# Each 128-row matmul with w_o as two 64-row matmuls side by side in the array

## The chip, the cores and the metric

The kernel runs on one core of a Trainium2 chip. The metric is the device time of one execution in microseconds, the median of several runs. Two kernels that differ by more than about 0.2% can be told apart.

## What is computed

The program is two layers of an encoder trunk over 640 tokens (512 of a new stream, 128 of eight running ones), model width 1024, in fp32. In each layer a half-step feed-forward block is followed by a mixer and a second feed-forward block. What matters here is the end of the mixer and what comes before and after it:

```python
m = g_conv * (y_conv @ w_conv_out) + g_attn * (y_attn @ w_attn_out)
x = x + m @ w_o                                  # the products of this change
x = x + 0.5 * swiglu(rmsnorm(x, norm_ffn2), w_ffn2_gu, w_ffn2_down)
```

## The kernel before

**Numbers.** Activations lie transposed: eight tiles `x[0..7]` of 128 channels x 640 tokens. To keep fp32 precision at the speed of the fp32r type, every operand is split into a rounded part and a remainder (`hi`, `lo`), and each product is three matmuls: hi x hi, lo x hi, hi x lo. The remainder of a weight block is made on VectorE (`wlo`, line 269) from a ScalarE cast (`whi`, line 264), two blocks ahead of its use. `flush()` issues the pending `wlo` subtractions.

**A product.** `steps` (line 327) takes one 128 x 128 weight tile per contraction step; `product` (line 341) runs all of them. With w_o there are 8 contraction steps, 3 terms and 2 token halves of 320 columns: 48 matmuls of 128 rows x 128 columns on 320 tokens (line 337). They accumulate in one PSUM tile `po` of two banks, a bank for each half. The eight output blocks m = 0..7 of a layer are eight such products, 384 matmuls a layer, 768 in all.

**PSUM.** From the gates of the mixer on (`layout(f"g{l}", 1)`, line 954) the eight banks are divided in two pools: `acc` with two buffers of two banks each, and `att` with four buffers of one bank. Each pool hands out its buffers in turn, and the first matmul into a buffer waits until the last reader of its previous content is done.

- The products with w_conv_out and w_attn_out (`out`, line 1071) take `acc` buffers in turn, as `py`; line 1081 reads them on VectorE.
- The products with w_o (lines 962 to 966) took `acc` buffers in turn as well, as `po`; line 966 adds a finished one to `x[m]` on VectorE.
- The three sums of the next block's first `gate_up` (line 709: `pa`, `pb`, `pc`) take `att` buffers.

**Order.** In these stages TensorE, VectorE and ScalarE each run their instructions in the order of the program. The last w_attn_out product is issued with its VectorE work in this order: the remainders of three operands for w_o (`give`, line 182, `m_3lo` to `m_5lo`), then line 1081, an add to `mm`, and the last two remainders `m_6lo`, `m_7lo`. Then follow, for each m, the product, `ex.weights(m)` (which prepares weights of the next block at m = 5 and 7), the add to `x[m]`, the `wlo` of a block two ahead, and `ex.final(m)`: the operands of the next block, made from `x[m]`: about two VectorE steps for an even m, five for an odd one (lines 481 to 514), their squares on ScalarE (line 533), and a running sum of squares (line 208). After m = 7 comes `gate_up`, whose first matmuls read operands of the even blocks, then of the odd ones; a little later the sum of squares is reduced on TensorE (line 427, `npsb`).

Elsewhere the kernel already has matmuls with 64 contraction rows: the attention scores (line 1207), where two heads lie in partitions 0 to 63 and 64 to 127, and each head has a PSUM bank of its own. They are plain fp32.

Of the kernel before, what the change touches and what calls it, by code (L numbers as in the profile page):

```python
# [13 lines left out]
ALU = mybir.AluOpType  # L14
# [9 lines left out]
HT = T // 2  # L24
PAST = 256
H = 8
HD = 64
# [106 lines left out]
def two(ps):  # L134
    return ps[:, :, :HT]


def halves(t):
    return t.rearrange("p (a b) -> p a b", a=2)
# [3 lines left out]
def trunk(ctx: ExitStack, tc: tile.TileContext, xin, wst, small, pbias, samplebias, kcache, vcache,  # L143
          yout, ko, vo, co):
    nc = tc.nc
    PE, DVE, ACT, POOL, SP = nc.tensor, nc.vector, nc.scalar, nc.gpsimd, nc.sync
# [8 lines left out]
    ps = ExitStack()  # L155
# [12 lines left out]
    def acc(name):  # L168
        return banks["acc"].tile([P, 2, 512], F32, tag="acc", name=name)

    def att(name):
        return banks["att"].tile([P, 512], F32, tag="att", name=name)
# [14 lines left out]
    slabs, n = [], 0  # L187
# [19 lines left out]
    def add(out, a, b):  # L207
        DVE.tensor_tensor(out=out, in0=a, in1=b, op=ALU.add)  # L208
# [58 lines left out]
    def flush():  # L267
        for lo, src, hi in pending:
            DVE.tensor_tensor(out=lo, in0=src, in1=hi.bitcast(F32), op=ALU.subtract)  # L269
        pending.clear()  # L270
# [50 lines left out]
    tiles = Tiles()  # L321
# [5 lines left out]
    def steps(ps, ops, at=()):  # L327


        n = len(ops)  # L330
        for k, (xh, xl) in enumerate(ops):
            if k in at:
                at[k]()
            wh, wl = tiles.take()
            for j, (w, x) in enumerate(((wh, xh), (wh, xl), (wl, xh))):
                for a in range(2):
                    PE.matmul(ps[:, a, :HT], w, x[:, a * HT : (a + 1) * HT],  # L337
                              start=k == 0 and j == 0, stop=k == n - 1 and j == 2)
            yield

    def product(ps, ops, at=()):
        for _ in steps(ps, ops, at):
            pass

    def block(ps, s, half, ops, ks, start, stop):

        for kp in ks:
            w = [z[:, (half * NP + kp) * P : (half * NP + kp + 1) * P] for z in s]
            xh, xl = ops(kp)
            for j, (a, b) in enumerate(((w[0], xh), (w[0], xl), (w[1], xh))):  # L350
                PE.matmul(ps, a, b, start=start and kp == 0 and j == 0,  # L351
                          stop=stop and kp == NP - 1 and j == 2, skip_group_check=True)
# [15 lines left out]
    x = [xp.tile([P, T], F32, name=f"x{k}") for k in range(KT)]  # L368
    for k in range(KT):
# [4 lines left out]
        if k % 2 == 0:  # L374
            c = slice(k * P, (k + 2) * P)
# [192 lines left out]
    def opening(fp, name, goff, n, put, tails):  # L568
# [52 lines left out]
        for i in range(2 * n):  # L621
            ps.append(acc(f"po{name}_{i}"))
            product(ps[i], h, at.get(i, {}))
            if i > 1:
                out(i - 1)
            if i == 0:
                for k in range(KT):
                    ex.square(k)
                    ex.add()
                    if k == 1:  # L630
                        out(0)
                    if k == 4:
                        flush()
            if i == 1:
                continue
            if i == 3:
                g, u = gs[0], us[0]
                DVE.tensor_tensor(out=g, in0=g, in1=ex.rho, op=ALU.mult)
                ACT.activation(g, g, AF.Silu)
                DVE.tensor_tensor(out=u, in0=u, in1=ex.rho, op=ALU.mult)  # L640
            flush()
            for m in made.get(i, ()):
                ex.final(m, False)
            if i == 3:
                DVE.tensor_tensor(out=u, in0=u, in1=g, op=ALU.mult)
            if i == max(made):
                ex.rest()
# [176 lines left out]
    def ffn(name, fp, ex, goff, after, end=False):  # L824
# [9 lines left out]
        for what, a in ffn_order(name):  # L834
            if what in ("std", "cut"):
                continue
            if what == "gu":
                turned = after is not None and not end
                gate_up(fp, f"{name}_{a}", ex, a == plain, turned, tails, act.__setitem__, a)
                continue  # L840
            js = a[0][1]
            if js[0] == last or len(a) * len(js) >= KT:
                for t in tails:
                    t()
                tails.clear()
            if after is not None and js[0] == last:
                nxt = nxt or after()
            if end and js[0] == last:
                nxt.all([act[j] for j in js])
                break  # L850
            for m, js in a:
                pd = acc(f"pd{name}_{js[0]}_{m}")
                product(pd, [act[j] for j in js])
                done = nxt and m == KT - 1
                if nxt:
                    nxt.weights(m)
                DVE.scalar_tensor_tensor(out=halves(x[m]), in0=two(pd), scalar=0.5,  # L857
                                         in1=halves(x[m]), op0=ALU.mult, op1=ALU.add)
                if not done:
                    flush()  # L860
                if nxt:
                    nxt.final(m)
# [5 lines left out]
    def mixer(l, after):  # L868
        with tc.tile_pool(name=f"yp{l}", bufs=1, reuse_waits="tile") as yp, \
# [8 lines left out]
            ops = Operands(l, op, h, ycs, [yas[:, c, :] for c in range(1, CT)])  # L878
# [76 lines left out]
            with tc.tile_pool(name=f"gp{l}", bufs=1, reuse_waits="tile") as gp, \  # L955
                 tc.manual_schedule(engines=ORDERED):
                hold[0] = True
                mo = outputs(l, gp, ops.X, st, cs, ycs, yas, sigmoid, gates)
        ex = after(st)
        with tc.manual_schedule(engines=ORDERED):  # L960
            hold[0] = True
            for m in range(KT):
                po = acc(f"po{l}_{m}")
                product(po, mo)
                ex.weights(m)
                DVE.tensor_tensor(out=halves(x[m]), in0=two(po), in1=halves(x[m]), op=ALU.add)
                if m < KT - 1:
                    flush()
                ex.final(m)
# [532 lines left out]
    for l in range(L):  # L1502
        if l == 0:
            open_pool("fp")
            ex = None
        with tc.manual_schedule(engines=ORDERED):
            ffn(f"a{l}", pool[0], ex, O_G1, None)
        fp.close()

        def after(st):  # L1510
            open_pool(f"fp{l}")
            return Expand(pool[0], f"b{l}", O_G2 + l * KT, st)

        ex = mixer(l, after)
        with tc.manual_schedule(engines=ORDERED):
            if l < L - 1:
                ex = ffn(f"b{l}", pool[0], ex, 0,
                         lambda: Expand(pool[0], f"a{l + 1}", O_G1 + (l + 1) * KT, ex))
            else:
                ffn(f"b{l}", pool[0], ex, 0, Final, True)  # L1520
# [128 lines left out]
```

## Time and profile before

| | us |
|---|---|
| median of 3 runs | 2574.79 (2574.21 to 2574.84) |
| the profiled execution | 2574.47 |
| its span, first to last instruction | 2572.7 |
| TensorE busy | 2553.6, 17576 matmuls |
| VectorE busy | 1934.1 |
| ScalarE busy | 1144.7 |
| matmuls with w_o on the chain that ended last | 4.0% of the span |

In rows of the time line the first number is the start in us from the beginning of the span and the second the length in us; then come the engine (PE is TensorE, PEld its weight loads, DVE VectorE, ACT ScalarE), line, operation, output and inputs, shape and count. A bracket gives the idle time of the engine before the row and what ended it. Rows of groups give the busy time of the group in us and the mean length in ns of one. A matmul's length includes its way through the array, so the next one starts well before it ends; the time that a stream of matmuls costs is read from start to start.

### The profile page before, as it was taken

How to read it: one execution, taken by the hardware profiler on the slowest of the kernel's cores; microseconds unless marked ns; L12 is line 12 of the kernel's file. 1: busy time of each engine (PE TensorE's matmuls, PEld its weight loads, DVE VectorE, ACT ScalarE, POOL GpSimd, SP SyncE). 2: the span in 40 equal slices, each digit the busy share in tenths (PEclk: the TensorE clock that was granted, in tenths of full speed). 3: DMA queues.
4: the chain of work that ended last, by engine and by line, in shares of the span. 5: the costliest groups of instructions: out<-in, count | busy, mean ns of one | idle time of the engine just before them, and what ended most of it. 6: DMA issues, size and time to landing. Idle time of an engine off the chain costs nothing.

```text
span 2572.7 us, 42534 instructions
## 1 busy us (share of the span) xinstructions
PE 2553.6 (99%) x17576; PEld 2497.1 (97%) x17576; DVE 1934.1 (75%) x2973; ACT 1144.7 (44%) x1802; POOL 60.5 (2%) x153
## 2 busy tenths in 40 slices
PE   8999999999999999999999999999999999999998
PEld 8999999888999999999999999998889999999998
DVE  7786767778777987677787767787786778777676
ACT  5343335575444543334444333356644445433333
POOL 0000000111000000000000000001110000000000
PEclk9999999999999999999999999999999999999999
DMA  3222223235222232222222222233442222222222
GB/s 133 66 100 91 81 75 108 99 116 168 75 83 88 74 102 74 81 89 78 83 82 99 74 90 83 74 101 113 134 136 83 74 91 81 92 83 74 91 91 74
DMA packets 74066, 237.05 MB, mean 92 GB/s; under 512 B 8241, under 2 KB 19121, under 8 KB 73873
## 3 DMA queue, kind: packets, MB, share of 16 engines
q1 hardware_dynamic: 70272, 223.90, 26.0%
q0 software_dynamic: 2880, 9.79, 1.1%
q8 instruction: 138, 2.26, 0.4%
q10 hardware_dynamic: 720, 0.65, 0.1%
q14 instruction: 56, 0.45, 0.1%
HBM read 225.85 MB, written 7.94 MB: 91 GB/s over the span
## 4 chain that ended last, share of the span: by engine, by line
PE 92%; DVE 4%; ACT 3%; issue 1%; DMA 0%; ACTq 0%; DVEq 0%
PE pab L351 12%; PE pda L337 12%; PE pdb L337 11%; PE paa L351 11%; PE pcb L351 6%; PE pca L351 5%; PE py L337 4%; PE po L337 4%; PE qa L351 4%; PE pbb L351 3%; PE pba L351 3%; PE pv L1160 2%; PE ma_cv L351 2%; PE ma_qk L351 2%; PE qc L351 2%; PE ma_b L351 1%
## 5 line engine op out<-in xcount | busy, mean ns | idle before, releaser
L269 DVE TENSOR_TENSOR wlo<-raw,whi 128x1024 fp32r<-128x1024 f32 (+2 forms) x540 | 562.5, 1047 | 189.5 <-ACT whi L264 187.3
L264 ACT CAST whi<-raw 128x1024 fp32r<-128x1024 f32 (+2 forms) x540 | 489.9, 912 | 253.7 <-PE pca L351 79.4
L351 PE MATMUL pab<-xhib,whi 128*128 128x320 f32 x704 | 218.4, 310 | 0.4 <-ACT u_b L791 0.4
L351 PE MATMUL pab<-xlob,whi 128*128 128x320 f32 x704 | 217.5, 309 | 0.0
L351 PE MATMUL pab<-xhib,wlo 128*128 128x320 f32 x704 | 217.5, 309 | 0.0
L351 PE MATMUL paa<-xhia,whi 128*128 128x320 f32 x640 | 198.2, 310 | 0.7 <-ACT c_a L727 0.5
L351 PE MATMUL paa<-xloa,whi 128*128 128x320 f32 x640 | 197.7, 309 | 0.0
L351 PE MATMUL paa<-xhia,wlo 128*128 128x320 f32 x640 | 197.7, 309 | 0.0
L337 PE MATMUL pda<-ahia,whi 128*128 128x320 f32 x704 | 160.3, 309 | 0.6 <-DVE x L857 0.6
L337 PE MATMUL pda<-ahia,wlo 128*128 128x320 f32 x704 | 160.4, 309 | 0.0
L337 PE MATMUL pda<-aloa,whi 128*128 128x320 f32 x704 | 160.4, 309 | 0.0
L264 ACT CAST whi<-s 128x1024 fp32r<-128x1024 f32 (+1 forms) x120 | 109.5, 912 | 111.8 <-DVE s L208 85.4
L337 PE MATMUL pdb<-ahib,wlo 128*128 128x320 f32 x656 | 149.5, 309 | 0.0
L337 PE MATMUL pdb<-alob,whi 128*128 128x320 f32 x656 | 149.4, 309 | 0.0
L337 PE MATMUL pdb<-ahib,whi 128*128 128x320 f32 x656 | 149.3, 309 | 0.0
L269 DVE TENSOR_TENSOR wlo<-s,whi 128x1024 fp32r<-128x1024 f32 (+1 forms) x120 | 127.2, 1060 | 13.1 <-ACT whi L264 13.1
L351 PEld LDWEIGHTS pab<-xhib,whi 128*128 128x128 f32 x704 | 132.2, 188 | 1.2 <-ACT u_b L791 0.9
L351 PEld LDWEIGHTS pab<-xlob,whi 128*128 128x128 f32 x704 | 132.2, 188 | 0.2
L351 PEld LDWEIGHTS pab<-xhib,wlo 128*128 128x128 f32 x704 | 132.1, 188 | 0.0
L351 PEld LDWEIGHTS paa<-xhia,whi 128*128 128x128 f32 x640 | 120.1, 188 | 1.3 <-ACT c_a L727 0.8
L351 PEld LDWEIGHTS paa<-xloa,whi 128*128 128x128 f32 x640 | 120.1, 188 | 0.1
L351 PEld LDWEIGHTS paa<-xhia,wlo 128*128 128x128 f32 x640 | 120.1, 188 | 0.0
(582 smaller groups left out, 6952.7 us busy)
## 6 DMA issues: line engine op xcount, KB each, us to landing
raw<-in_wst SPq DMA_DIRECT2D x384, 512.0 KB, 3.5
kc<-in_kcache SPq DMA_DIRECT2D x32, 256.0 KB, 4.0
vc<-in_vcache SPq DMA_DIRECT2D x16, 512.0 KB, 4.5
bias<-in_pbias POOLq DMA_DIRECT2D x16, 256.0 KB, 3.2
x<-in_xin SPq DMA_DIRECT2D x8, 320.0 KB, 5.1
out_vo<-v POOLq DMA_DIRECT2D x10, 256.0 KB, 2.5
out_ko<-k POOLq DMA_DIRECT2D x8, 320.0 KB, 2.5
out_yout<-x SPq DMA_DIRECT2D x8, 192.0 KB, 1.9
```

What stands on the lines that cost most here:

```text
L264: ACT.copy(hi[:, d], src[:, c])
L269: DVE.tensor_tensor(out=lo, in0=src, in1=hi.bitcast(F32), op=ALU.subtract)
L337: PE.matmul(ps[:, a, :HT], w, x[:, a * HT : (a + 1) * HT], start=k == 0 and j == 0, stop=k == n - 1 and j == 2)
L351: PE.matmul(ps, a, b, start=start and kp == 0 and j == 0, stop=stop and kp == NP - 1 and j == 2, skip_group_check=True)
L1160: PE.matmul(pv[t], xx[:, t * P : (t + 1) * P], w[:, kk * AW : (kk + 1) * AW], start=c == 0 and kk == 0 and j == 0, stop=c == KT // 2 - 1 a ...
```

## The change

Each matmul of a w_o product becomes two. The first uses weight rows 0 to 63 and the token operand's partitions 0 to 63, the second rows 64 to 127 of both. They lie beside each other in the array, and each has a sum of its own: four PSUM banks for an output block (two row halves x two token halves) in place of two. Even blocks take both `acc` buffers, odd blocks all four `att` buffers. Both sums are added to `x[m]`: two adds of 640 columns for an even block, four of 320 for an odd one, in place of one of 640.

```diff
+    def beside(ps, ops):
+        n = len(ops)
+        for k, (xh, xl) in enumerate(ops):
+            wh, wl = tiles.take()
+            for j, (w, x) in enumerate(((wh, xh), (wh, xl), (wl, xh))):
+                for a in range(2):
+                    for r in range(2):
+                        c = slice(r * HD, (r + 1) * HD)
+                        PE.matmul(ps[r][a], w[c], x[c, a * HT : (a + 1) * HT],
+                                  start=k == 0 and j == 0, stop=k == n - 1 and j == 2)
...
             for m in range(KT):
-                po = acc(f"po{l}_{m}")
-                product(po, mo)
+                if m % 2:
+                    po = [[att(f"po{l}_{m}_{r}{a}")[:, :HT] for a in range(2)] for r in range(2)]
+                else:
+                    pair = [acc(f"po{l}_{m}_{r}") for r in range(2)]
+                    po = [[z[:, a, :HT] for a in range(2)] for z in pair]
+                beside(po, mo)
                 ex.weights(m)
-                DVE.tensor_tensor(out=halves(x[m]), in0=two(po), in1=halves(x[m]), op=ALU.add)
+                for r in range(2):
+                    if m % 2:
+                        for a in range(2):
+                            add(halves(x[m])[:, a], po[r][a], halves(x[m])[:, a])
+                    else:
+                        add(halves(x[m]), two(pair[r]), halves(x[m]))
                 if m < KT - 1:
                     flush()
                 ex.final(m)
```

## The prediction

> **What bounds the kernel now.** I read the page's busy times and its chain first.
>
> ```profile
> span 2572.7 us, 42534 instructions
> PE 2553.6 (99%) x17576; PEld 2497.1 (97%) x17576; DVE 1934.1 (75%) x2973; ACT 1144.7 (44%) x1802; POOL 60.5 (2%) x153
> PE 92%; DVE 4%; ACT 3%; issue 1%; DMA 0%; ACTq 0%; DVEq 0%
> ```
>
> TensorE is busy 99% and makes 92% of the chain of waits. So time that the change costs TensorE, in streaming or in waiting, comes out at the end almost in full: no later idle time can take it up. Next, one product with w_o, by its starts on the time line (layer 0: products 0, 1; what follows product 7), and how long one matmul streams, by groups kept apart by shape.
>
> ```profile
> 802.92 0.46 PE L337 MATMUL po<-m_0hi,whi 128*128 128x320 f32 x2
> 803.21 0.46 PE L337 MATMUL po<-m_0lo,whi 128*128 128x320 f32 x2
> 810.42 0.46 PE L337 MATMUL po<-m_0hi,whi 128*128 128x320 f32 x2
> 859.70 0.31 PE L351 MATMUL pab<-xhib,whi 128*128 128x320 f32 x1
> ...
> L337 PE MATMUL po<-m_0hi,whi 128*128 128x320 f32 x32 | 7.3, 309 | 0.0
> L1160 PE MATMUL pv<-wlo,hhim 128*128 128x512 f32 x80 | 31.2, 390 | 0.0
> L1207 PE MATMUL pss<-k,q 64*128 64x512 f32 x32 | 8.2, 589 | 0.0
> L1207 PE MATMUL pss<-k,q 64*128 64x384 f32 x32 | 6.5, 484 | 0.0
> L1327 PE MATMUL spy<-vc,ss 128*32 128x128 f32 x256 | 10.3, 279 | 0.0
> ```
>
> Products 1 to 7 take 859.70 - 810.42 = 49.28 us, 7.04 each, so 147 ns for each of 48 matmuls. Of this, streaming is (390 - 309) / (512 - 320) = 0.42 ns a column, 135 ns for 320 columns; some 12 ns are overhead.
>
> **The matmuls: beside each other, or not.** 768 matmuls become 1536. The scores (`pss`) show 64-row matmuls of two heads in banks of their own. Their stream is (589 - 484) / 128 = 0.82 ns a column, so a 512-column record needs 0.42 us. A score of a pair of heads is two records for each head (32 records = 2 layers x 4 pairs x 2 heads x 2): eight groups of four. One behind the other, a group would be busy 3 x 0.42 + 0.59 = 1.85 us, eight of them 14.8. Two by two it is 0.42 + 0.59 = 1.01, eight of them 8.1. The row says 8.2: **they run two by two**, and the second of a pair costs nothing that can be seen. I take the same for the new pairs: 147 ns a pair, **0** for the doubled count. The bounds: the pair sheds the overhead, -12 ns x 768 = -9 us; each half brings its own, +12 x 768 = +9 us. The row nearest (pairs without any surcharge) speaks for 0. Not shown by any row: two banks written at once at fp32r's 0.42 ns a column (the scores write at half that rate). Issue I cost at nothing: two loads and two matmuls in 147 ns are 37 ns each, and the 256 matmuls of `spy` with their loads pass in 10.3 us, 20 ns each.
>
> [...] Here, where every load has the row group of the matmul before it, loads are hidden already: an exposed one lengthens the row of the 808.84 start below from 0.46 to 0.56 us, and 0.10 + 0.135 does not fit in 147 ns. [...]
>
> Entering and leaving the 64-row form costs something:
>
> ```profile
> 490.41 0.31 PE L351 MATMUL ma_qk<-hhim,wlo 128*128 128x320 f32 x1
> 490.65 1.17 PEld L1207 LDWEIGHTS pss<-k,q 64*128 64x128 f32 x12 [0.19 <-DVE wlo L269]
> 490.65 2.43 PE L1207 MATMUL pss<-k,q 64*128 64x128 f32 x16
> ```
>
> 490.41 to 490.65 is 0.24 us in place of 0.147. Once in and once out of each layer's stage: about **0.2 us a layer**.
>
> **First wait: the second accumulator.** Block 0 now needs both `acc` buffers. The buffer of its second row half is the one that the last `py` product leaves, and line 1081 reads that late. VectorE in this stretch, then the same in layer 1 with its products' starts:
>
> ```profile
> 801.44 0.82 DVE L1081 TENSOR_TENSOR g<-py,g 128x640 f32<-128x640 f32 x1
> 802.29 0.82 DVE L208 TENSOR_TENSOR mm<-mm,g 128x640 f32<-128x640 f32 x1
> 803.03 1.22 DVE L269 TENSOR_TENSOR wlo<-raw,whi 128x1024 fp32r<-128x1024 f32 x1
> 804.17 0.82 DVE L182 TENSOR_TENSOR m_3lo<-yc,m_3hi 128x640 fp32r<-128x640 f32 x1
> ...
> 806.37 0.82 DVE L1081 TENSOR_TENSOR g<-py,g 128x640 f32<-128x640 f32 x1
> 807.23 0.83 DVE L208 TENSOR_TENSOR mm<-mm,g 128x640 f32<-128x640 f32 x1
> 807.97 0.82 DVE L182 TENSOR_TENSOR m_6lo<-mm,m_6hi 128x640 fp32r<-128x640 f32 x1
> ...
> 808.84 0.56 PE L337 MATMUL po<-m_6lo,whi 128*128 128x320 f32 x2 [0.18 <-DVE m_6lo L182]
> ...
> 2076.89 0.82 DVE L1081 TENSOR_TENSOR g<-py,g 128x640 f32<-128x640 f32 x1
> ...
> 2073.10 0.46 PE L337 MATMUL po<-m_0hi,whi 128*128 128x320 f32 x2
> ...
> 2080.94 0.46 PE L337 MATMUL po<-m_0hi,whi 128*128 128x320 f32 x2
> ```
>
> The first buffer (line 1081 at 801.44) is free in time. The second is free at 806.37 + 0.82 = 807.19; the 808.84 row starts 0.05 after the `m_6lo` that it waits for, so the matmul of the second row half starts at 807.24. Before, that buffer was not asked for until product 1 at 810.42. VectorE does not come sooner: nothing in its queue here waits for `po`. Behind the waiting matmul stands all of TensorE's queue. From 807.24, 48 pairs take 7.04 us: product 1 starts at 814.28 in place of 810.42. The wait for `m_6lo` goes (ready at 808.79, now asked for some 5 us later): that is inside the difference. **+3.86 us.** Layer 1: 2076.89 + 0.82 + 0.05 + 7.04 = 2084.80 in place of 2080.94, **+3.86** too.
>
> **Second wait: VectorE's adds and the `att` banks.** The next block's `pa` takes the `att` buffer that came first in block 7, and its first matmul (859.70 above) must wait for the first add of block 7. Before, those banks were idle. How late is that add? VectorE between the products:
>
> ```profile
> 838.78 0.82 DVE L966 TENSOR_TENSOR x<-po,x 128x640 f32<-128x640 f32 x1 [0.75 <-PE po L337]
> ...
> 844.22 0.69 DVE L208 TENSOR_TENSOR s<-raw 128x512 f32<-128x512 f32 x1 [0.36 <-DMA raw<-in_wst]
> 845.82 0.82 DVE L966 TENSOR_TENSOR x<-po,x 128x640 f32<-128x640 f32 x1 [0.18 <-PE po L337]
> ...
> 852.86 0.82 DVE L966 TENSOR_TENSOR x<-po,x 128x640 f32<-128x640 f32 x1 [0.75 <-PE po L337]
> 853.60 1.22 DVE L269 TENSOR_TENSOR wlo<-raw,whi 128x1024 fp32r<-128x1024 f32 x1
> ...
> 860.20 0.82 DVE L966 TENSOR_TENSOR x<-po,x 128x640 f32<-128x640 f32 x1
> 861.05 0.89 DVE L481 SCALAR_TENSOR_TENSOR xob<-x,sm,rrm 128x640 f32<-128x640 f32 x1
> ...
> 866.68 1.68 DVE L208 TENSOR_TENSOR ssumb<-ssumb,sqb 128x640 f32<-128x640 f32 x2
> 868.27 0.48 DVE L208 TENSOR_TENSOR ub<-pbb,c_b 128x320 f32<-128x320 f32 x1
> 868.67 0.68 DVE L269 TENSOR_TENSOR wlo<-raw,whi 128x512 fp32r<-128x512 f32 x1
> ```
>
> From start to start an add of 640 takes 0.74 (852.86 to 853.60), 0.85 if the next one needs it (801.44 to 802.29), one of 320 takes 0.40 (868.27 to 868.67). So an even block adds 0.85 us, an odd one 4 x 0.40 - 0.74 = 0.86. Idle time takes up the early ones; block 3 leaves 0.86 - 0.75 = 0.11 for block 4. Then: block 5 starts 0.11 + 0.85 - 0.36 - 0.18 = 0.42 late, block 6 0.42 + 0.86 - 0.75 = 0.53, block 7, before which VectorE has no idle time, 0.53 + 0.85 = 1.38. Its first add ends at 860.20 + 1.38 + 0.48 = 862.06, and `pab` starts at 862.11 in place of 859.70: **+2.41 us** a layer. `pb` and `pc` take the second and third add's banks, which are free before their turn.
>
> What hangs on the later adds is covered by this wait. They shift VectorE by 1.38 + 3 x 0.40 + 0.52 - 0.85 = 2.25 us from 861.05 on, TensorE by 2.41. The sum of squares (866.68) is on the same queue and just in time for the reduction now; without the wait for `pa` it would cost 2.25 itself. The remainders `wlo` come up to 1.4 us later but are made some 5 us ahead.
>
> **The sum.** A layer 3.86 + 2.41 + 0.19 = 6.46, two layers 12.9 us. From the profiled execution's 2574.47 (span 2572.7 and 1.8 around it; the median of the runs is 0.3 higher): **2587.4 us**, 0.5% slower.
>
> **Rivals.**
> *One behind the other.* If fp32r pairs can't write two banks at full rate, each of the 768 added matmuls takes its own 147 ns: +113 us. Products of 14 us give VectorE room, so the second wait is only the add itself, 0.16 + 0.05 + 0.48 = 0.7; 2 x (3.86 + 0.7 + 0.2) more: 2697. The scores speak against it, at half the rate. If instead two halves side by side can't hide their loads, each pair waits 0.10 us more (the 808.84 row): 77 us, and 2661. Together 8%.
>
> *The clock falls in the first wait.* TensorE stands still 4.3 us. At the start, after 6 us of idleness, it is slow:
>
> ```profile
> 6.01 0.90 PE L337 MATMUL poa<-hhia,whi 128*128 128x320 f32 x2 [6.01 <-ACT whi L584]
> 7.33 0.73 PE L337 MATMUL poa<-hhia,wlo 128*128 128x320 f32 x2
> 7.87 0.73 PE L337 MATMUL poa<-hhia,whi 128*128 128x320 f32 x2
> ...
> 12.41 0.46 PE L337 MATMUL poa<-hhia,whi 128*128 128x320 f32 x2
> ```
>
> Two matmuls in 0.54 us (7.33 to 7.87) until about 12 us: 267 ns in place of 147. A repeat costs up to 6 x (1 - 147 / 267) = 2.7 us a layer: 2590 if one layer is hit, 2593 if both. 23%, since the wait is nearer to the 6 us that shows it than to a gap like the 0.18 us in the 808.84 row, which doesn't. [...]
>
> *Surcharge on each half*: +9 us, of which VectorE's wait gives back some 2: 2594. 7%.
>
> *The other side: faster.* If the two row halves keep separate streams and loads, the overhead goes, 12 ns x 768 pairs: -9 us. It decides from 12.9 / 768 = 17 ns a pair on, more than the 12 ns of overhead, and shorter products make the second wait longer. So it gives about 2580 unless a wait is absent too, about 2572 without the first one. [...] Against: the scores show no gain. 3% for faster, 4% for within 0.2%.
>
> **Numbers.** Forecast as summed, with a spread of 3 us: 55%; the others as given. Range 2580 to 2600: from the overhead shed to the surcharge with a slow clock. About 0.2% (5 us) is what the measurement can tell from no change. Faster 3%, same 4%, slower 93%.
>
> **What will show it.** Right: products 1 to 6 still 7.04 us; a wait of 4.3 us of `po` for `g` (line 1081) in each layer; one of 2.4 of `pab` for `x`. Wrong: products near 14 us; 267 ns a pair after the first wait; a start of the second half's matmul before line 1081 has read its bank.

## The result, and the profile after

The changed kernel takes **2594.59 us** (median, 2592.78 to 2594.81), the kernel before 2574.82 beside it: **1.0076 times** (95% interval 1.0058 to 1.0093). The forecast was 2587.4 in a range of 2580 to 2600. The sign and both waits were right; the likeliest case was 7 us short.

The page after, busy times and chain:

```profile
span 2591.0 us, 44122 instructions
PE 2560.1 (99%) x18344; PEld 2503.2 (97%) x18344; DVE 1947.1 (75%) x3005; ACT 1145.8 (44%) x1802; POOL 61.1 (2%) x153
PE 90%; DVE 6%; ACT 3%; issue 1%; DMA 0%; DVEq 0%; ACTq 0%
```

The profiled execution took 2592.78 us, 18.3 more than the one before. 768 more matmuls added only 6.5 us to TensorE's busy time (over 5 of them by the slow clock below), and VectorE's share of the chain rose from 4% to 6%: the time went into waits. On TensorE's time line the stage looks like this (layer 0; the fifth row is product 1, the sixth product 2, the last two the end of product 7 and the next block):

```profile
802.62 0.41 PE L354 MATMUL po<-m_0hi,whi 64*128 64x320 f32 x1
806.85 0.90 PE L354 MATMUL po<-m_0hi,whi 64*128 64x320 f32 x3 [3.82 <-DVE g L1103]
807.28 0.99 PE L354 MATMUL po<-m_0lo,whi 64*128 64x320 f32 x4
...
816.32 0.60 PE L354 MATMUL po<-m_7hi,wlo 64*128 64x320 f32 x4
816.61 0.60 PE L354 MATMUL po<-m_0hi,whi 64*128 64x320 f32 x4
...
823.65 0.45 PE L354 MATMUL po<-m_0hi,whi 64*128 64x320 f32 x3
...
865.60 0.60 PE L354 MATMUL po<-m_7hi,wlo 64*128 64x320 f32 x4
868.65 0.38 PE L363 MATMUL pab<-xhib,whi 128*128 128x320 f32 x1 [2.46 <-DVE x L208]
```

The two VectorE rows that end the waits:

```profile
805.97 0.82 DVE L1103 TENSOR_TENSOR g<-py,g 128x640 f32<-128x640 f32 x1
...
868.02 1.68 DVE L208 TENSOR_TENSOR x<-po,x 128x320 f32<-128x320 f32 x4
```

Four things are to be seen. Product 1 takes 823.65 - 816.61 = 7.04 us: twice the matmuls in the same time, so each pair takes the 147 ns of one matmul before. TensorE waits from 802.62 to 806.85 for the last read of the second accumulator (line 1081 of before is 1103 here; it ends at 806.79). It waits again before `pab`, for the first add of block 7 (868.02). And product 0 takes 816.61 - 802.62 = 14.0 us, though its wait is only 4.1: the four matmuls from 807.28 on, two pairs, last 0.99 us, and the four from 816.61 on only 0.60. The granted clock in four stretches of 3.41 us, half of the 6.83 us that this slow piece lasts (806.18 to 813.00), says why:

```profile
802.74:806.15 3.41, 0.28 (x1) 0.06 (x1) 3.41 (x5) 1.41 (x2) 0.00 (x0) 1.00 0.34 79
806.15:809.57 3.42, 2.72 (x20) 2.73 (x22) 3.03 (x4) 0.72 (x1) 0.00 (x0) 0.50 0.18 74
809.57:812.98 3.41, 3.41 (x30) 3.41 (x28) 0.00 (x0) 0.00 (x0) 0.00 (x0) 0.50 0.00 0
812.98:816.39 3.41, 3.41 (x50) 3.41 (x48) 0.00 (x0) 0.00 (x0) 0.00 (x0) 1.00 0.02 5
```

The columns after the stretch's length are busy time (and count) of TensorE, its weight loads, VectorE, ScalarE and GpSimd, then the clock. It is 0.50 for two stretches after the idle one, and pairs take 267 ns there. From 806.85 on the product takes 9.76 us (to 816.61) where product 1 takes 7.04: some 2.7 us a layer go to the clock.

| us more than before | layer 0 | layer 1 |
|---|---|---|
| product 0 (14.0 in place of 7.50 and 7.84) | 6.5 | 6.2 |
| wait before `pab` | 2.6 | 2.6 |

Together 17.9 of the 18.3.

### The profile page after: what moved, and what is told of

Same layout as the page of the kernel before. It is cut to its first block, busy times and chain, and to the rows that moved or that the text cites. A ratio compares the mean times of both kernels' runs of the same rounds, so it can differ in the third digit from the quotient of the medians.

```text
span 2591.0 us, 44122 instructions
## 1 busy us (share of the span) xinstructions
PE 2560.1 (99%) x18344; PEld 2503.2 (97%) x18344; DVE 1947.1 (75%) x3005; ACT 1145.8 (44%) x1802; POOL 61.1 (2%) x153
## 4 chain that ended last, share of the span: by engine, by line
PE 90%; DVE 6%; ACT 3%; issue 1%; DMA 0%; DVEq 0%; ACTq 0%
PE pab L363 12%; PE pda L337 11%; PE pdb L337 11%; PE paa L363 11%; PE pcb L363 6%; PE pca L363 5%; PE py L337 4%; PE qa L363 4%; PE pbb L363 3%; PE pba L363 3%; PE po L354 2%; PE pv L1182 2%; PE ma_cv L363 2%; PE ma_qk L363 2%; PE qc L363 2%; DVE wlo L269 1%
```

## The experiments

The theory: two waits for PSUM buffers, the slow clock after the first one, and VectorE's extra adds behind the second; the pairs themselves cost nothing. The main rival: the 64-row form costs something in itself, or its entry lowers the clock. The times of before beside these runs are medians of 2574.5 to 2575.2.

### swap: the buffers exchanged

```diff
-                if m % 2:
+                if m % 2 == 0:
                     po = [[att(...
...
-                    if m % 2:
+                    if m % 2 == 0:
                         for a in range(2):
```

> Even blocks take the four att buffers, odd ones both acc buffers: nothing else changes. Theory (the changed kernel pays for two buffer waits and for the slow clock after the first): both waits of PE for a buffer go, the clock stays, product 0 takes 7.5 to 7.8 us again; what is left is VectorE's lateness after block 7, which now reaches TensorE itself, about 2.1 us a layer, and 0.2 for the change of form: 2574.5 + 4.6 = 2579. Rival (64-row pairs cost something in themselves, or entering their form lowers the clock): 2585 or more, product 0 still near 14 us.

Measured: 2580.02, 1.0021 times before (1.0011 to 1.0030). Still all blocks as pairs, still the same adds, and three quarters of the loss is gone. Product 0 takes 7.41 us (802.67 to 810.08) and `pab` starts right behind product 7. What is left waits for VectorE:

```profile
859.45 0.41 PE L363 MATMUL pab<-xhib,whi 128*128 128x320 f32 x1
...
866.42 0.41 PE L363 MATMUL pbb<-xlob,whi 128*128 128x320 f32 x1 [0.25 <-DVE xlob L526]
867.91 0.42 PE L363 MATMUL pab<-xlob,whi 128*128 128x320 f32 x1 [0.78 <-DVE xlob L526]
869.04 0.42 PE L363 MATMUL pcb<-xhib,wlo 128*128 128x320 f32 x1 [0.28 <-DVE wlo L269]
```

The kernel before had that last matmul, and the `wlo` that it needs, at

```profile
865.54 1.22 DVE L269 TENSOR_TENSOR wlo<-raw,whi 128x1024 fp32r<-128x1024 f32 x1
...
867.04 0.31 PE L351 MATMUL pcb<-xhib,wlo 128*128 128x320 f32 x1
```

From the first `pab` to it pass 869.04 - 859.45 = 9.59 us, and 867.04 - 859.70 = 7.34 before: 2.25 us in this layer, the three waits with the change of form (2.23 in layer 1). That is 4.5 of swap's 5.1. The rival falls: the pairs can be had without the two waits and without the slow clock.

### first_whole: only the first wait taken away

```diff
-                    pair = [acc(f"po{l}_{m}_{r}") for r in range(2)]
+                    pair = [acc(f"po{l}_{m}_{r}") for r in range(2 if m else 1)]
...
-                beside(po, mo)
+                if m:
+                    beside(po, mo)
+                else:
+                    product(pair[0], mo)
...
-                for r in range(2):
+                for r in range(2 if m else 1):
```

> Block 0 of each layer goes back to 48 matmuls of 128 rows in one acc buffer, the other seven blocks stay as pairs. Theory: the first wait and its slow clock go (product 0 back to 7.5 and 7.8 us), the wait of pab for the first add of block 7 stays at 2.6 us: 2574.5 + 2 x (2.6 + 0.2) = 2580. Rival (the pairs' form lowers the clock on entry): product 1 now shows 267 ns a pair, 2585 or more.

Measured: 2581.52 (1.0026; 1.0016 to 1.0035). Entering the form in product 1, behind a busy TensorE, keeps the clock:

```profile
802.40:809.90 7.50, 7.32 (x50) 6.97 (x48) 6.69 (x9) 2.39 (x3) 0.00 (x0) 1.00 0.25 70
809.90:816.90 7.00, 7.00 (x96) 6.89 (x96) 3.25 (x4) 2.42 (x3) 0.00 (x0) 1.00 0.28 77
```

96 matmuls in 7 us at 1.00: the form doesn't lower it. The wait before `pab` is still there (862.33, 2.77 us idle).

### fill26: the wait kept, the idleness taken away

26 matmuls that compute nothing that is used are put where TensorE waits.

```diff
+                if m == 0:
+                    z, fil = mo[0][0], att(f"fill{l}")[:, :HT]
+                    for i in range(26):
+                        PE.matmul(fil, z[:, :P], z[:, :HT], start=True, stop=True)
                 beside(po, mo)
```

> The changed kernel with 26 more 128-row matmuls per layer (3.8 us) into an att bank that nobody reads, issued where TensorE waits for the second accumulator. The wait for line 1081's read still ends at the same time. Theory (idleness of 4.2 us lowers the clock for 6 us): the pairs after it take 147 ns from the start, product 0 from its first pair 11.1 us in place of 14.0 counted with the filling, 2 x 2.9 less: 2587 to 2589. Rival (the slow pairs belong to entering the form or to the wait itself): no gain, 2593 to 2595, pairs still 267 ns.

Measured: 2590.14 (1.0057; 1.0042 to 1.0072), from 2588.36 to 2591.1. More work, and 4.5 us less than the change. From the first pair to product 1 (806.77 to 814.18) now pass 7.41 us. VectorE was as late as ever, so this 4.5 is the price of the clock after the first wait, as far as the rest is equal; 2 x (9.76 - 7.41) = 4.7 from the two traces agrees. The rest is not quite equal: in this profiled execution (2591.1) the clock was also at half after both waits before `pab` (866.2 to 869.6 and 2146.2 to 2149.6), which the first trace of the change didn't have.

### read_early: the first wait made shorter

```diff
             product(py, y)
-            if then:
+            late = m == 2 * KT - 1
+            if then and not late:
                 then()
...
                 add(mm[m - KT], mm[m - KT], g)
+            if then and late:
+                then()
             flush()
```

> The last w_attn_out product is read on VectorE (line 1081 of before) ahead of the remainders m_3lo to m_5lo in place of after them. Theory: the first wait shrinks from 4.2 to about 2.1 us, shorter than the 2.7 us before pab that left the clock alone, so the slow pairs go too: 2592.8 - 2 x (2.1 + 2.9) = 2583. Rival (any wait of some us, or the form, lowers the clock): only 2 x 2.1 less, 2588.5, with slow pairs left.

Measured: 2586.84 (1.0043; 1.0028 to 1.0058), from 2583.93 to 2587.99: between theory and rival. The wait did shrink to 2.0 us from start to start. But my "2.7 us is harmless" fell: in the profiled execution the wait of 2.0 in layer 0 lowered the clock, the same wait in layer 1 didn't. Product 0 took 10.56 us in layer 0 and 9.03 in layer 1, so this fall of the clock cost 1.5. Stretches of 3.413 us, laid so that their borders meet the ends of this execution's slow pieces (first two rows layer 0, the others layer 1):

```profile
803.18:806.59 3.41, 1.79 (x17) 1.38 (x17) 3.38 (x4) 1.67 (x2) 0.00 (x0) 1.00 0.11 18
806.59:810.00 3.41, 3.41 (x28) 3.41 (x28) 3.41 (x6) 0.73 (x1) 0.00 (x0) 0.50 0.36 136
2079.70:2083.10 3.40, 2.66 (x17) 2.25 (x16) 3.37 (x5) 2.86 (x5) 0.00 (x0) 1.00 0.01 4
2083.10:2086.50 3.40, 2.52 (x34) 2.52 (x36) 3.37 (x6) 1.12 (x2) 0.00 (x0) 1.00 0.46 154
```

In layer 0 the whole wait lies in one stretch, in layer 1 it is cut in two. That gave a new theory, of windows on a fixed grid.

### after_again: the grid, foretold

The changed kernel, unaltered, for a second trace.

> The changed kernel once more, for a second trace. Theory from five traces (the clock is set by windows of a fixed grid of 3.413 us: one in which TensorE stands still for more than about 1.9 us halves the next one's clock): both waits of 4.2 us are followed by 267 ns a pair; a wait of 2.7 before pab is so only if over 1.9 us of it lie in one window, counted in steps of 3.413 us from the end of the slow stretch at the program's start; all ends of slow stretches lie whole multiples of 3.413 apart. Rival (a fixed threshold of idle time between 2.8 and 4.2): never after the waits before pab. Time 2592 to 2596, 1.3 to 1.7 more for each slow stretch after pab's wait.

Measured: one time, 2593.43. The slow pieces end at 11.55 (the start), 810.27, 871.71, 2090.27 and 2151.71: 234.0, 252.0, 609.0 and 627.0 times 3.413 after the first. Both waits before `pab` (2.8 and 2.6 us) lie whole in one window here, and both are followed by the slow clock. The first of them:

```profile
864.85:868.26 3.41, 0.82 (x7) 0.59 (x6) 3.41 (x6) 1.04 (x1) 0.00 (x0) 1.00 0.00 0
868.26:871.67 3.41, 3.41 (x15) 3.41 (x15) 2.78 (x6) 1.60 (x3) 0.00 (x0) 0.51 0.00 0
871.67:875.08 3.41, 3.41 (x25) 3.41 (x25) 3.12 (x4) 1.51 (x3) 0.00 (x0) 0.99 0.00 0
```

The same wait in the first trace of the change (2.6 us, to 868.65) was cut by a border at 867.62, 16 windows after the end of the slow piece at 813.00, and the clock stayed at 1.00. Hence executions of one program can differ by some us (2592.78 to 2594.81 here). That it explains the 1.8 us between the median and the profiled execution is likely but argued, since the others have no trace.

### swap_to_5 and swap_to_5b: VectorE's adds

Swapped parity, blocks 6 and 7 whole. In swap_to_5 both sum in `acc`; in swap_to_5b block 6 sums in two `att` banks. The core of the second:

```diff
+                if m == 6:
+                    pair = [[att(f"po{l}_{m}_{a}")[:, :HT] for a in range(2)]]
+                elif m == 7:
+                    pair = [acc(f"po{l}_{m}")]
+                elif m % 2 == 0:
                     po = [[att(...
...
+                if m == 6:
+                    entire(pair[0], mo)
+                elif m == 7:
+                    product(pair[0], mo)
+                else:
+                    beside(po, mo)
```

> The swapped parity, and blocks 6 and 7 back to whole matmuls with one add each. Theory (what swap still lost is VectorE's extra adds just before the next block): block 7's add is only about 0.5 us late, 0.4 a layer reaches TensorE, 0.2 a layer for the change of form: 2574.8 + 1.2 = 2576. Rival (the pairs cost by their number): three quarters of swap's loss of 5.1 stays, 2578.6.

Measured: 2578.81 (1.0015; 1.0006 to 1.0024), what the rival had said, but not for its reason. Block 6 asked for the buffer that block 5 had just filled:

```profile
847.52 0.54 PE L337 MATMUL po<-m_0hi,whi 128*128 128x320 f32 x2 [1.81 <-DVE x L208]
```

I had built a third wait of the kind in question. Hence the second kernel:

> As swap_to_5 (pairs for blocks 0 to 5 in the swapped parity, whole matmuls for 6 and 7), but block 6 sums in two att banks and block 7 in an acc buffer, so that neither takes a buffer that the block just before it used. Theory (swap_to_5 lost 2 us a layer to such a buffer, and swap its time to VectorE's extra adds before the next block): no wait above 1 us is left, 0.4 a layer from VectorE's lateness, 0.2 a layer for the change of form: 2574.6 + 1.2 = 2576. Rival (pairs cost by their number, three quarters of swap's 5.1): 2578.5.

Measured: 2576.77 beside 2575.17, 1.0006 times (0.9998 to 1.0015). Three quarters of the pairs remain and the loss is no longer clear of zero; the rival's 2578.5 lies above every one of the 11 times. So the pairs don't cost by their number. That the adds cost only where the next block is about to need what is queued behind them fits this and swap's three waits.

### six_by_six and half_by_half: when two run beside each other

In each contraction step the six matmuls of one row half come first, then the six of the other:

```diff
-            for j, (w, x) in enumerate(((wh, xh), (wh, xl), (wl, xh))):
-                for a in range(2):
-                    for r in range(2):
+            for r in range(2):
+                for j, (w, x) in enumerate(((wh, xh), (wh, xl), (wl, xh))):
+                    for a in range(2):
```

> The same pairs in another order: in each contraction step first the six matmuls of rows 0 to 63, then the six of rows 64 to 127. Theory (matmuls start in program order; two run beside each other only if they are neighbours of different row halves): of 12 matmuls of a step only the one at each border has a partner, 10 slots of 147 ns in place of 6, products of 11.8 us, 16 x 4.7 = 75 us more, less 2 x 1.9 of the wait before pab, as VectorE has more time: about 2665. Rival (the array overlaps them in any order): 7.04 us a product, 2593. Rival (never two at once): 14.1 us a product, 2700.

Measured: 2591.76. My theory was 73 us off. Operand 4's matmuls of the one half run while the other half is still at operand 3, and products stay at 7.04 us:

```profile
826.20 0.31 PE L354 MATMUL po<-m_3lo,whi 64*128 64x320 f32 x1
826.32 0.31 PE L354 MATMUL po<-m_4hi,whi 64*128 64x320 f32 x1
826.35 0.31 PE L354 MATMUL po<-m_3lo,whi 64*128 64x320 f32 x1
826.47 0.30 PE L354 MATMUL po<-m_4hi,whi 64*128 64x320 f32 x1
```

So matmuls of different row halves don't have to be neighbours. How far ahead can one get? The same with all 48 of a half first:

```diff
+        ws = [tiles.take() for _ in ops]
+        for r in range(2):
+            c = slice(r * HD, (r + 1) * HD)
+            for k, ((xh, xl), (wh, wl)) in enumerate(zip(ops, ws)):
                 ...
```

> The changed kernel with all 48 matmuls of rows 0 to 63 of a block first, then the 48 of rows 64 to 127. Theory after six_by_six (each row half runs as a stream of its own, and starts ahead of the other's queue): if the streams have no limit to how far one runs ahead, products stay at 7.04 us and the time at 2592 to 2596. Rival (it can run ahead only by a queue of limited length, fewer than 48 matmuls with their loads): part of each product runs with one half of the array alone, products of 8 to 14 us, 2610 to 2700.

Measured: 2673.14, products of 13.1 us. The border between two halves (the last four of operand 7, and what runs beside them):

```profile
829.77 0.31 PE L354 MATMUL po<-m_7lo,whi 64*128 64x320 f32 x1
829.78 0.41 PE L354 MATMUL po<-m_0hi,whi 64*128 64x320 f32 x1
829.92 0.31 PE L354 MATMUL po<-m_7lo,whi 64*128 64x320 f32 x1
830.03 0.30 PE L354 MATMUL po<-m_0hi,whi 64*128 64x320 f32 x1
830.07 0.31 PE L354 MATMUL po<-m_7hi,wlo 64*128 64x320 f32 x1
830.17 0.31 PE L354 MATMUL po<-m_0lo,whi 64*128 64x320 f32 x1
830.21 0.31 PE L354 MATMUL po<-m_7hi,wlo 64*128 64x320 f32 x1
830.32 0.31 PE L354 MATMUL po<-m_0lo,whi 64*128 64x320 f32 x1
```

The other half starts 7 ns after the fourth matmul from the end of the first half, ahead of the last three. There are two such borders to a product (halves of 6.56 us). At each, four matmuls run beside four: 96 matmuls take 96 - 2 x 4 = 88 places, 88 x 0.147 = 12.9. In six_by_six, with runs of six, this reach was enough.

### before_wlo_late and before_wlo_after: a version ahead of both

The kernel before waits for `m_6lo` in product 0, behind a `wlo` that is not needed until product 1.

```diff
                 add(mm[m - KT], mm[m - KT], g)
-            flush()
+            if m != 2 * KT - 2:
+                flush()
```

In before_wlo_after the condition is `if m < 2 * KT - 2`.

> The kernel before, with one wlo subtraction moved behind the operands of w_o (the flush after the last but one w_attn_out product is left out, so that it is issued with the first w_o product). Theory: the wait of product 0 for m_6lo (0.35 us in layer 0, 0.7 in layer 1) goes, since VectorE reaches m_6lo and m_7lo 1.1 us sooner; the wlo is needed only in product 1: 1.0 us less, 2573.8. Rival (another operand is late in its place, or the wlo): no change, 2574.8 or more.

Measured: 2575.01, 1.0002 times (0.9993 to 1.0011): nothing. The next flush issued the `wlo` five VectorE instructions later, still ahead of `m_6lo`. With both left out:

> The kernel before, with the wlo subtraction now behind all operands of w_o (the flush is left out after both last w_attn_out products; leaving out one only moved it by four places, still ahead of m_6lo). Theory: m_6lo and m_7lo are ready 1.1 us sooner, product 0's wait for them goes (0.35 and 0.7 us): 2574.6 - 1.0 = 2573.6. Rival (the operand's ScalarE half or the wlo itself is late then): 2574.6 or more.

Measured: 2574.02 beside 2575.17, 0.9996 times (0.9987 to 1.0005). Its span is 2571.3, and the wait is gone from the trace (in the kernel before, `m_6lo` starts at 808.84 after idleness):

```profile
808.16 0.46 PE L337 MATMUL po<-m_6lo,whi 128*128 128x320 f32 x2
```

About 1 us, as forecast, and not certain by the times alone.

## Why the prediction was right, and where its size was off

- **Two 64-row matmuls take the time of one**: right to the nanosecond (7.04 us a product). The unknown that I kept open, two banks written at full rate, costs nothing, the overhead of 12 ns is neither shed nor doubled, and no pair waits for its loads.
- **The first wait**, forecast from line 1081 and the order of buffers: right. 4.1 us of idleness in each layer where 4.3 stood, ended by the instruction named.
- **The second wait**: right in place and cause, 2.6 us for 2.41. Block 7's add came 1.5 us late, counted from the end of product 7, for 1.38.
- **What hangs on the later adds is covered by this wait**: right, as swap shows from the other side. Without the wait for `pab`, 2.25 us, the change of form among them, reach TensorE, about the size that the forecast gave. But they reach it at two operands (`xlob`) and at a `wlo`, ahead of the sum of squares that it named. And that `wlo` was not made some 5 us ahead: before, it was done at 866.76 and first used at 867.04, 0.3 us later. The wait for `pab` hid this error.
- **The step that failed is the choice of the likeliest case**, without the fall of the clock, which stood as a rival at 23% with a time of 2593 if both layers were hit. Both were, and in two traces out of two; fill26 prices it at 4.5 us, the first trace at 2 x 2.7 = 5.4. By as much the profiled execution's 2592.78 lies above 2587.4. The slow pieces of after_again end whole multiples of 3.413 us apart. The 23% weighed 4.3 us between the 6.0 of the start and a gap of 0.18; apart from the start, the longest wait of TensorE in the trace of before is 1.0 us. Here 1.9 us of idleness within one window of 3.413 us were enough (a busy share of about 45%: 1.5 of 3.413), and 4.1 us always hold that much in one of two windows. I also left out that the wait of 2.6 can be hit.

## What to carry to other kernels

When a change makes an output take twice the buffers, look up who held each of them last and when it is read: the price is in the order of the buffers, and changing the order alone gave back three quarters of it. If a wait stops TensorE for 2 us or more, price the half clock after it as well: here the waits of 4.2 us had it behind them in both layers of both traces of the change, those of 2.0 us in one layer of read_early, and it cost some 1.5 us for one slow window, 2.7 for two. Splitting a full 128-row matmul by rows gained nothing here (fp32r, 320 columns): the halves side by side take the whole one's 147 ns.

## What the runs showed of the hardware that was not expected

- **The clock's windows.** A slow piece lasted 3.41 us (868.3 to 871.7 in after_again) or twice that (806.18 to 813.00 in after), at a clock of 0.50. Seven of the traces (after, after_again, six_by_six, read_early, fill26, first_whole, swap_to_5) have waits of TensorE of 2.0 to 4.2 us from start to start, 22 in all. Count as idle what lies between 0.135 us after the last start and the next start. Then the next window was slow whenever 1.89 us or more of idleness lay within one window of 3.413 us (12 waits), and never up to 1.83 (10 waits, cut by a border). Between the two lies the border in these traces. A slow window was followed by another when it held 0.64 us or more of idleness itself (three cases), and by full speed at 0.55 or less. At the program's start the clock column reads 1.00 while matmuls take 267 ns: there the spacing is what decides.
- **Order within the array.** A matmul on one row half started ahead of up to three earlier ones of the other half (826.32 in six_by_six, 829.78 in half_by_half); my theory ahead of six_by_six had them start in the order of the program.
